# Matmuls moved into the waits of five norms, and one unit for both context query tiles in differential attention

## The chip, the cores and the metric

The kernel runs on one NeuronCore of a Trainium2 chip, in one launch. The metric is device time in microseconds, the median over runs; less is better. The engines are TensorE (PE in the rows: matmuls, with PEld for its weight loads), VectorE (DVE), ScalarE (ACT), GpSimd (POOL) and SyncE (SP), which issues most DMAs. A matmul accumulates in a PSUM bank; the other engines read it from there.

## The reference

Two transformer layers in sequence over a latent `h` of 256 tokens by 1024, all in float32. The first block is a convolution and retention mixer, a feed-forward part and a gated projection of a side input `p`, each closed by an RMS norm that is added to the residual:

```
x = x + rmsnorm(concat(y_conv, y_ret) @ w_out, mix_post_norm)
h = rmsnorm(x, ffn_pre_norm)
x = x + rmsnorm((silu(h @ w_ffn_gate) * (h @ w_ffn_up)) @ w_ffn_down, ffn_post_norm)
e = sigmoid(x @ w_ple_gate) * (p @ w_ple_proj)
x = x + rmsnorm(e, ple_post_norm)
```

The second block has two layers over the latent and over a context of 256 tokens, each with a modulated norm, attention, and a SwiGLU. Its first layer is differential attention with 8 heads of two 64-wide score maps; the latent's queries see context and latent keys (512), the context's queries see the context's keys (256):

```
p = softmax(q1 k1) - lam * softmax(q2 k2)          # per head, per query
y = rmsnorm(p @ v, subln) * (1 - lam_init) @ wo
h = h + g_m * y;  h = h + g_f * swiglu(modulate(rmsnorm(h)))   # and the same for ctx
```

The second layer is neighbourhood attention with 16 heads of 64 over the latent, followed by the same kind of SwiGLU and a last norm.

## The kernel before

**Matmuls.** Every float32 weight block is loaded by SP (`raw`), and split into two rounded parts: `hi` by a cast on ACT (L130), `lo` by a subtraction on DVE (L131). The buffers of `hi` and `lo` are five each, of 1024 columns. Activations are split in the same way. A product is then three matmuls, hi·hi, hi·lo and lo·hi, for each of its 8 blocks of 128 rows (`mm3`, L169 to L171; with tokens on the output's partitions `mm3_tok`, L196 to L198). 24 matmuls make one 128x256 output, 48 a bank of 512 columns.

**Norms.** A norm over 1024 features runs across partitions. `Stat.add` squares a tile on ACT (L226, L229) and adds it on DVE (L231). `rstd` sums over partitions by matmuls with a column of ones (L242), scales on DVE (L212), raises to the power -1/2 on POOL (L213), and broadcasts the result over the partitions by matmuls (L248). `post_norm` then makes, for each of 8 tiles, a product and a sum on DVE (L553, L554), a hi part on ACT (L148 or L152) and a lo part on DVE (L149 or L153), on which the next matmuls wait. `norm_mod` does the same with a modulation (DVE L639, ACT L642, DVE L643).

**Order.** The instructions are written in Python in program order; the framework's scheduler orders each engine's queue and places waits. `tc.issue_after(ins)` holds what is written in its block behind `ins` in that order. Around the change, the program goes: input products; `pp`, the product of `p` with `w_ple_proj` (48 matmuls, 12 for each of four banks of the ring `mm`, copied out at L531); the output projection `w_out` (192 matmuls); its norm; the feed-forward part; three blocks of the second layer's `wqkv` for the context (`early_some(0, 3)`, 48 matmuls each); `post_norm` into `o`; the gate `w_pg` (192 matmuls) with the product `e`; the `early` rest; the norm of `e`; the norm of layer two; then differential attention.

**Differential attention.** `da_unit` handles one tile of 128 queries of one head: two score maps in two PSUM banks (L781, 64 rows of weights), a maximum over each (DVE L788), an exponential with its sum (ACT L790), a reciprocal and two combinations on DVE (L794 to L796), transposes (L799), a copy (L801), the product with v (L806), and a norm of its own with ACT and POOL (L809 to L813). 8 heads have 2 latent and 2 context units each, 32 in all. Between units, `fill_in` places projection pieces of the next heads. The next unit's scores wait until both banks are free (`both_free`).

**After attention.** `wo_piece` and `wo_rest` apply the output projection for latent (v=0) and context (v=1) and add to the residual (L958); `ffn_norm` and `ffn_first` are the norm and the first four banks of the following SwiGLU (24 matmuls for each bank and v).

**Neighbourhood attention.** At L1119 each of 8 pairs of heads multiplies probabilities with values in 8 pairs of matmuls that use 64 columns of the array each, over four blocks of keys.

Of the kernel before, what the change touches and what calls it, by code (L numbers as in the profile page):

```python
# [14 lines left out]
P = 128  # L15
# [19 lines left out]
EARLY = 3, 3  # L35
# [27 lines left out]
def body(ctx, tc, a):  # L63
# [151 lines left out]
    class Stat:  # L215
# [5 lines left out]
        def add(self, src):  # L221
# [13 lines left out]
        def rstd(self, r=None, columns=False, keep=True):  # L235
# [11 lines left out]
            for t in range(nt):  # L247
                pe.matmul(pb[:, t * P:(t + 1) * P], v[:, t:t + 1].to_broadcast([P, P]), ident, start=True, stop=True)  # L248
# [171 lines left out]
    sm = tmp1("sm", 1)  # L420
# [144 lines left out]
    def out_proj(name, xs, base):  # L565
# [3 lines left out]
        for c in range(4):  # L569
# [24 lines left out]
    for j in range(KF):  # L594
        w = w_blocks(a["ffn1"][j])
# [77 lines left out]
    def early_qk(c, grp):  # L673
# [695 lines left out]
```

## Time and profile before

| | |
|---|---|
| median of 3 runs | 1416.42 us (1415.89 to 1419.45) |
| the profiled execution's own time | 1422.92 us |
| its span, first to last instruction | 1421.1 us |
| mean granted TensorE clock | 0.983 |
| PE busy | 1377.3 us, 97% |
| DVE busy | 1077.5 us, 76% |
| ACT busy | 698.6 us, 49% |
| POOL busy | 66.8 us, 5% |
| DMA | 239.76 MB, mean 169 GB/s |

The chain of work that ended last runs over PE for 91% of the span. The profile's 40 slices show PE busy nine tenths or more nearly everywhere; the stretches below that are short, and a table of 20 us stretches shows them better than the slices do. A row of the trace gives start and duration in us, the engine, line and operation, and in brackets the idle time before it with what ended it. One matmul's duration overlaps the next one's; the distance between starts is what it costs.

### The profile page before, as it was taken

What the parts mean: (1) busy time and instruction counts of PE and PEld (TensorE: products, weight loads), DVE (VectorE), ACT (ScalarE), POOL (GpSimd) and SP (SyncE); (2) the same over time, 40 slices, a digit from 0 to 9 for tenths busy, and PEclk for the clock granted to TensorE, in tenths of its full rate; (3) what the DMA queues carried; (4) which work ended last, traced back from release to release, by engine and by line L of the source; (5) the groups of instructions that cost most, each with busy time, mean ns of one, the idle gap of its engine ahead of it and who ended that gap; (6) DMA issues with size and microseconds to landing.
All of it is one profiled execution on the core that took longest, in us unless ns stands there. A gap on an engine that the chain in (4) does not pass through costs nothing.

```text
span 1421.1 us, 24831 instructions
## 1 busy us (share of the span) xinstructions
PE 1377.3 (97%) x9465; PEld 1240.0 (87%) x9465; DVE 1077.5 (76%) x2198; ACT 698.6 (49%) x1323; POOL 66.8 (5%) x119
## 2 busy tenths in 40 slices
PE   6999899999998999999999999999999999999997
PEld 6899799999997899799888888888997878888886
DVE  6875799986576788977699999974754556797764
ACT  5656544454365778664422222223544445655442
POOL 0000000000000223220000000000000000000000
PEclk9999899999999999999999999999999999999999
DMA  8356498667354234234465676643632223455563
GB/s 287 113 185 226 172 321 295 221 206 223 132 195 159 94 121 129 80 103 163 133 219 182 210 250 216 213 143 109 192 131 87 93 80 116 135 191 190 157 179 98
DMA packets 78311, 239.76 MB, mean 169 GB/s; under 512 B 8816, under 2 KB 14192, under 8 KB 78064
## 3 DMA queue, kind: packets, MB, share of 16 engines
q1 hardware_dynamic: 77760, 237.79, 51.8%
q8 instruction: 74, 1.21, 0.4%
q10 hardware_dynamic: 432, 0.39, 0.1%
q14 instruction: 45, 0.37, 0.1%
HBM read 237.10 MB, written 1.05 MB: 168 GB/s over the span
## 4 chain that ended last, share of the span: by engine, by line
PE 91%; DVE 2%; ACT 2%; DMA 2%; issue 1%; POOL 1%; SPq 0%; POOLq 0%; ACTq 0%; DVEq 0%
PE mm L169 20%; PE mm L170 19%; PE mm L171 19%; PE mm L181 5%; PE s L181 2%; PE mm L183 2%; PE mm L196 2%; PE mm L197 2%; PE mm L198 2%; PE s L781 1%; PE o L1119 1%; PE s L171 1%; PE s L170 1%; PE s L169 1%; PE t L806 1%; PE s L1079 1%
## 5 line engine op out<-in xcount | busy, mean ns | idle before, releaser
L130 ACT CAST hi<-raw 128x1024 fp32r<-128x1024 f32 (+2 forms) x382 | 365.1, 958 | 514.8 <-PE mm L170 280.5
L131 DVE TENSOR_TENSOR lo<-raw,hi 128x1024 fp32r<-128x1024 f32 (+2 forms) x382 | 422.6, 1108 | 170.3 <-ACT hi L130 166.0
L169 PE MATMUL mm<-x,hi 128*128 128x256 f32 (+2 forms) x1444 | 454.8, 319 | 15.8 <-ACT x L152 7.8
L170 PE MATMUL mm<-x,hi 128*128 128x256 f32 (+2 forms) x1444 | 454.2, 316 | 1.4 <-DVE x L643 1.3
L171 PE MATMUL mm<-x,lo 128*128 128x256 f32 (+2 forms) x1444 | 453.3, 315 | 0.8 <-DVE lo L131 0.8
L169 PEld LDWEIGHTS mm<-x,hi 128*128 128x128 f32 x1444 | 278.7, 195 | 45.1 <-issue 16.0
L171 PEld LDWEIGHTS mm<-x,lo 128*128 128x128 f32 x1444 | 280.5, 194 | 18.4 <-issue 3.4
L170 PEld LDWEIGHTS mm<-x,hi 128*128 128x128 f32 x1444 | 280.7, 195 | 17.6 <-issue 1.7
L282 DVE SCALAR_TENSOR_TENSOR junk<-adaw,sb 128x512 f32<-128x512 f32 x320 | 220.2, 688 | 11.8 <-DMA adaw<-ada 7.3
L169 PE MATMUL mm<-o,hi 128*128 128x256 f32 (+1 forms) x284 | 84.9, 306 | 2.3 <-ACT o L148 2.1
L171 PE MATMUL mm<-o,lo 128*128 128x256 f32 (+1 forms) x284 | 85.9, 304 | 0.0
L170 PE MATMUL mm<-o,hi 128*128 128x256 f32 (+1 forms) x284 | 85.7, 303 | 0.0
L213 POOL TENSOR_TENSOR rv<-rv,mhalf 128x2 f32<-128x2 f32 (+1 forms) x16 | 14.5, 906 | 1203.5 <-DVE rv L212 1203.5
L196 PE MATMUL mm<-hi,x 128*128 128x256 f32 x240 | 70.1, 292 | 0.0
L198 PE MATMUL mm<-hi,x 128*128 128x256 f32 x240 | 69.1, 288 | 0.0
L197 PE MATMUL mm<-lo,x 128*128 128x256 f32 x240 | 68.9, 287 | 0.0
L170 PE MATMUL mm<-q,hi 128*128 128x256 f32 (+1 forms) x195 | 61.2, 314 | 0.0
L171 PE MATMUL mm<-q,lo 128*128 128x256 f32 (+1 forms) x195 | 61.1, 313 | 0.0
L169 PE MATMUL mm<-q,hi 128*128 128x256 f32 (+1 forms) x195 | 61.1, 313 | 0.0
L169 PEld LDWEIGHTS mm<-o,hi 128*128 128x128 f32 x284 | 54.2, 194 | 6.0 <-ACT o L148 2.8
L171 PEld LDWEIGHTS mm<-o,lo 128*128 128x128 f32 x284 | 55.2, 194 | 2.5 <-issue 0.8
L170 PEld LDWEIGHTS mm<-o,hi 128*128 128x128 f32 x284 | 55.2, 194 | 1.7
(288 smaller groups left out, 2386.9 us busy)
## 6 DMA issues: line engine op xcount, KB each, us to landing
raw<-gu SPq DMA_DIRECT2D x88, 512.0 KB, 4.5
adaw<-ada SPq DMA_DIRECT2D x80, 512.0 KB, 4.5
raw<-wqkv SPq DMA_DIRECT2D x72, 512.0 KB, 4.0
raw<-ffn SPq DMA_DIRECT2D x44, 512.0 KB, 5.5
raw<-down SPq DMA_DIRECT2D x37, 384.0 KB, 3.2
raw<-down SPq DMA_DIRECT2D x37, 320.0 KB, 3.0
raw<-w_in SPq DMA_DIRECT2D x22, 512.0 KB, 5.2
o<-ada SPq DMA_DIRECT2D x32, 256.0 KB, 5.7
```

The source lines that it names most:

```text
L130: last_conv[:] = [act.copy(hi[:, :n], raw[:, :n]).ins, dve.tensor_tensor(lo[:, :n], raw[:, :n], f32(hi[:, :n]), op=ALU.subtract).ins]
L131: dve.tensor_tensor(lo[:, :n], raw[:, :n], f32(hi[:, :n]), op=ALU.subtract).ins]
L169: pe.matmul(out, wh, xh, start=first and k == 0, stop=False)
L170: pe.matmul(out, wh, xl, start=False, stop=False)
L171: last_mm[0] = pe.matmul(out, wl, xh, start=False, stop=last and k == n - 1).ins
L181: last_mm[0] = pe.matmul(out, wh, x, start=first and k == 0, stop=end).ins
L183: last_mm[0] = pe.matmul(out[:, :T], wl, x[:, :T], start=False, stop=False).ins
L196: pe.matmul(out, xh[:, ts_], wh, start=k == 0, stop=False)
L197: pe.matmul(out, xh[:, ts_], wl, start=False, stop=False)
L198: pe.matmul(out, xl[:, ts_], wh, start=False, stop=k == n - 1)
L213: pool.tensor_tensor(out, out, mhalf[:, :n], op=ALU.pow)
L282: dve.scalar_tensor_tensor(out=junk, in0=raw[:, gs_], scalar=1.0, in1=sb[:, v, gs_], op0=ALU.mult, op1=ALU.mult, accum_out=acc[:, n, v, g: ...
```

## The change

Four edits. First, `rstd` takes a pair `fill`: one function is called behind the sum matmuls, one behind the broadcast matmuls, and each writes matmuls there. Second, work is cut and handed to it: `pp` into four pieces of 12 matmuls, moved from before `w_out` to behind it; the 9 context blocks of `wqkv` into 36 quarters of 12, dealt out by `FILLS`; the pieces of `wo` for v=1 and of `ffn_first(0)`. Third, `da_unit` takes one or two query tiles: the two context tiles of a head become one unit with 512 columns per bank. Fourth, the order of the key blocks and of the two heads at L1119 is reversed. `w_pp` now keeps 2 of the 5 weight buffers from the input products until the norm behind `w_out`, and the first two `ffn1` blocks are written behind that projection's last square and sum.

```diff
+FILLS = 6, 1, 5, 3, 1, 12, 1, 5, 99
@@ Stat.rstd
+            if fill:
+                fill[0](mm.ins)
             v = small.tile([P, 4], F32, tag="rv", name="rv", bufs=4)
             inv_sqrt(v[:, :nt], ps[:, :nt], 1.0 / self.of)
...
+            if fill:
+                fill[1](mm.ins)
@@ after the input products
-    w = per_k(weights(a["w_pp"], (1024, 1024)), (8, 8), P)
...
-    for c in range(4):
-        ps = bank(pmm, "mm")
-        for j in range(2):
-            n = 2 * c + j
-            mm3(ps[:, j * T:(j + 1) * T], w[2 * n:2 * n + 2], px)
-        s = slot("pt")
-        act.activation(s, ps, AF.Copy, scale=0.5)
-        pp.append(s)
+    w_pp = per_k(weights(a["w_pp"], (1024, 1024)), (8, 8), P)
@@ behind out_proj
+    def pp_piece(ins):
+        c = len(pp)
+        ps = bank(pss, "s")
+        with behind(ins):
+            for j in range(2):
+                n = 2 * c + j
+                mm3(ps[:, j * T:(j + 1) * T], w_pp[2 * n:2 * n + 2], px)
...
     blocks, st = out_proj("w_out", ys, V_MIXPOST)
-    xs, st = post_norm(blocks, st, "x", V_FFNPRE)
+    pp_piece(last_mm[0])
+    xs, st_x = post_norm(blocks, st, "x", V_FFNPRE, (pp_piece, lambda ins: [pp_piece(ins) for _ in range(2)]))
+
+    with tc.issue_after(st.last_sq), tc.issue_after(st.last_add):
+        w_next = [w_blocks(a["ffn1"][j]) for j in range(2)]
@@ before post_norm "o", and the two norms behind it
-    early_some(0, EARLY[0])
+    fill(FILLS[0])(None)
+    xs, _ = post_norm([blocks[n // 2][:, (n % 2) * T:(n % 2 + 1) * T] for n in range(KD)], st, "o",
+                      fill=(fill(FILLS[1]), fill(FILLS[2])))
...
-        early_some(EARLY[0], EARLY[1])
-    r = st.rstd(keep=False)
+    fill(FILLS[3])(last_mm[0])
+    r = st.rstd(keep=False, fill=(fill(FILLS[4]), fill(FILLS[5])))
...
-    r = st.rstd(keep=False)
+    r = st.rstd(keep=False, fill=(fill(FILLS[6]), fill(FILLS[7])))
-    early_some(EARLY[1] if EARLY[1] is not None else EARLY[0], 99)
@@ da_unit (qts is (0,), (1,) for the latent, (0, 1) for the context)
-            dve.tensor_reduce(out=sc[:, 2 + m:3 + m], in_=o, axis=AX.X, op=ALU.max, negate=True)
+            dve.tensor_reduce(out=nmax[:, m, :nq], in_=ps[m].rearrange("p (u n) -> p u n", u=nq), axis=AX.X, op=ALU.max, negate=True)
             e = tmp2("e", 3)
-            act.activation(e[:, :n], o, AF.Exp, bias=sc[:, 2 + m:3 + m], accum_out=sc[:, 4 + m:5 + m])
+            for u in range(nq):
+                us = slice(u * n, (u + 1) * n)
+                act.activation(e[:, us], ps[m][:, us], AF.Exp, bias=nmax[:, m, u:u + 1], accum_out=sums[:, m, u:u + 1])
@@ behind attention
-    ffn_norm(0)
-    wo_first(1)
+    wo_some(1, (0, 1))(None)
+    ffn_norm(0, (wo_some(1, (2,)), wo_some(1, (3, 4, 5, 6, 7))))
...
-    ffn_first(0)
-    ffn_norm(1)
-    ffn_first(1)
+    ffn_first(0, (0,))(None)
+    ffn_norm(1, (ffn_first(0, (1,)), ffn_first(0, (2, 3))))
+    ffn_first(1, (0, 1, 2, 3))(None)
@@ na_heads
-            for kt in range(4):
-                for jj in range(2):
+            for kt in (3, 2, 1, 0):
+                for jj in (1, 0):
```

PE's queue at the norm behind `w_out`, before: `mm_1673` is the last bank of `w_out`, `t` the norm's two small products, `mm_1872` the first bank of the feed-forward part.

```order
L171 MATMUL mm_1673<-x_1449,lo_1668 128x256
L242 MATMUL t_1730<-ones_100,acc_1514 128x1 x2
L242 MATMUL t_1730<-ones_100,sq_1727 128x1 x2
L248 MATMUL t_1738<-tab_98,rv_1735 128x128 x2
L169 MATMUL mm_1872<-x_1744,hi_1860 128x256
```

The same place in the changed kernel, with four pieces of `pp` (`s_1670`, `s_1690`, `s_1711`, `s_1726`), of 12 matmuls each:

```order
L171 MATMUL s_1670<-x_1152,lo_1349 128x256
L245 MATMUL t_1685<-ones_100,acc_1454 128x1 x2
L245 MATMUL t_1685<-ones_100,sq_1666 128x1 x2
L169 MATMUL s_1690<-x_1152,hi_1348 128x256
...
L254 MATMUL t_1708<-tab_98,rv_1705 128x128 x2
L169 MATMUL s_1711<-x_1152,hi_1354 128x256
...
L169 MATMUL s_1726<-x_1152,hi_1354 128x256
...
L169 MATMUL mm_1884<-x_1744,hi_1811 128x256
```

One piece stands ahead of the sum, one between sum and broadcast, two behind the broadcast.

DVE's queue at the same norm, before, from the last weight part to the norm's first finished tile:

```order
L131 TENSOR_TENSOR lo_2023<-raw_2024,hi_2022 128x1024
L231 TENSOR_TENSOR acc_1514<-acc_1514,sq_1723 128x256
L212 TENSOR_SCALAR rv_1735<-t_1730 128x2
L553 TENSOR_TENSOR t1_1741<-q_1465,t_1738 128x256
L553 TENSOR_TENSOR t1_1749<-q_1465,t_1738 128x256
L554 TENSOR_TENSOR h0_85<-h0_85,t1_1741 128x256
L554 TENSOR_TENSOR h1_86<-h1_86,t1_1749 128x256
L153 SCALAR_TENSOR_TENSOR x_1744<-h0_85,vec_97,x_1744 128x256
```

And in the changed kernel:

```order
L234 TENSOR_TENSOR acc_1454<-acc_1454,sq_1663 128x256
L215 TENSOR_SCALAR rv_1705<-t_1685 128x2
L131 TENSOR_TENSOR lo_1812<-raw_1813,hi_1811 128x1024
L131 TENSOR_TENSOR lo_1818<-raw_1819,hi_1817 128x1024
L550 TENSOR_TENSOR t1_1741<-q_1405,t_1708 128x256
L550 TENSOR_TENSOR t1_1749<-q_1405,t_1708 128x256
L131 TENSOR_TENSOR lo_1824<-raw_1825,hi_1823 128x1024
L551 TENSOR_TENSOR h0_85<-h0_85,t1_1741 128x256
L551 TENSOR_TENSOR h1_86<-h1_86,t1_1749 128x256
L131 TENSOR_TENSOR lo_1830<-raw_1831,hi_1829 128x1024
L153 SCALAR_TENSOR_TENSOR x_1744<-h0_85,vec_97,x_1744 128x256
```

The weight parts of the feed-forward blocks, before the norm's sum until now, stand between the norm's own steps; a fifth one, `lo_2023`, follows four tiles later.

PE's queue from the norm of `e` to layer two's first products, before (`acc_4809` is the sum for `e`, `acc_5037` that for layer two, `x_5091` its first normed tile):

```order
L170 MATMUL s_5206<-x_3965,hi_5194 128x256
L242 MATMUL t_5023<-ones_100,acc_4809 128x1 x2
...
L248 MATMUL t_5031<-tab_98,rv_5028 128x128 x2
L196 MATMUL s_5269<-hi_5257,x_3935 128x256
...
L242 MATMUL t_5080<-ones_100,acc_5037 128x1 x2
...
L248 MATMUL t_5088<-tab_98,rv_5085 128x128 x2
L169 MATMUL mm_5526<-x_5091,hi_5520 128x256
```

In the changed kernel (`x_5443` is the first normed tile):

```order
L171 MATMUL s_5023<-x_3950,lo_5031 128x256
L245 MATMUL t_5072<-ones_100,acc_4809 128x1 x2
...
L254 MATMUL t_5094<-tab_98,rv_5091 128x128 x2
L169 MATMUL s_5097<-x_3935,hi_5098 128x256
...
L245 MATMUL t_5332<-ones_100,acc_5289 128x1 x2
L169 MATMUL s_5337<-x_3935,hi_5338 128x256
...
L254 MATMUL t_5365<-tab_98,rv_5362 128x128 x2
L169 MATMUL s_5337<-x_3955,hi_5338 128x256
...
L169 MATMUL mm_5500<-x_5443,hi_5494 128x256
```

The first sum moved from behind 68 matmuls (two blocks and 20 of the second) to behind 36; behind the second broadcast stand now 60 matmuls (`s_5337`, 36, and `s_5406`, 24), where before `mm_5526` followed at once.

## Rows read from the trace of the kernel before

**Rows 1.** the page's busy time: us, share of the span, instructions
```profile
PE 1377.3 (97%) x9465; PEld 1240.0 (87%) x9465; DVE 1077.5 (76%) x2198; ACT 698.6 (49%) x1323; POOL 66.8 (5%) x119
```

**Rows 2.** busy us by 20 us stretch: length, engines with their instructions, PEclk, DMA
```profile
140.00:160.00 20.00, 13.79 (x89) 13.28 (x90) 13.02 (x34) 9.58 (x25) 0.69 (x1) 0.74 0.34 137
...
360.00:380.00 20.00, 17.22 (x128) 16.84 (x127) 10.67 (x19) 8.16 (x12) 0.69 (x1) 0.85 0.50 165
...
440.00:460.00 20.00, 14.97 (x104) 13.83 (x105) 15.98 (x34) 10.14 (x18) 0.00 (x0) 0.90 0.41 128
...
640.00:660.00 20.00, 20.00 (x169) 19.95 (x168) 18.42 (x38) 11.63 (x20) 0.57 (x1) 1.00 0.68 232
...
660.00:680.00 20.00, 17.86 (x125) 17.48 (x124) 10.31 (x25) 4.96 (x11) 0.70 (x1) 0.83 0.18 58
```

**Rows 3.** the timeline, w_out's inputs to normed tiles: start, us, what, [idle, releaser]
```profile
112.68 1.23 ACT L515 ACTIVATE pt<-t,rv 128x128 f32<-128x128 f32 x4
...
139.41 0.28 PE L171 MATMUL mm<-x,lo 128*128 128x256 f32 x1
...
140.61 1.04 ACT L130 CAST hi<-raw 128x1024 fp32r<-128x1024 f32 x1 [1.97 <-DMA raw<-ffn]
...
141.69 1.23 DVE L131 TENSOR_TENSOR lo<-raw,hi 128x1024 fp32r<-128x1024 f32 x1 [1.79 <-ACT hi L130]
...
143.39 0.98 PE L242 MATMUL t<-ones,acc 128*128 128x1 f32 x4 [3.70 <-DVE acc L231]
...
146.33 1.23 PE L248 MATMUL t<-tab,rv 128*128 128x128 f32 x4 [1.10 <-POOL rv L213]
...
149.27 1.01 PE L169 MATMUL mm<-x,hi 128*128 128x256 f32 x3 [1.72 <-ACT x L152]
...
158.49 0.48 DVE L153 SCALAR_TENSOR_TENSOR x<-h,vec,x 128x256 fp32r<-128x256 f32 x1 [0.24 <-ACT x L152]
```

**Rows 4.** the timeline of PE at post_norm into o
```profile
374.08 1.22 PE L248 MATMUL t<-tab,rv 128*128 128x128 f32 x4 [1.16 <-POOL rv L213]
...
376.92 1.01 PE L169 MATMUL mm<-o,hi 128*128 128x256 f32 x3 [1.61 <-ACT o L148]
```

**Rows 5.** the timeline from w_pg's last matmul to attention's first scores
```profile
401.67 0.28 PE L171 MATMUL mm<-o,lo 128*128 128x256 f32 x1
...
406.98 0.42 DVE L231 TENSOR_TENSOR acc<-acc,sq 128x256 f32<-128x256 f32 x1
...
440.75 0.50 PE L169 MATMUL mm<-x,hi 128*128 128x256 f32 x2 [1.58 <-ACT x L642]
...
442.79 0.58 PE L170 MATMUL mm<-x,hi 128*128 128x256 f32 x1 [1.29 <-DVE x L643]
...
457.82 0.50 PE L781 MATMUL s<-o 64*128 64x512 f32 x2 [2.44 <-ACT o L148]
```

**Rows 6.** the timeline at the norm of the context behind attention
```profile
663.28 0.48 DVE L643 SCALAR_TENSOR_TENSOR x<-t,mod,x 128x256 fp32r<-128x256 f32 x1
...
668.64 0.16 DVE L212 TENSOR_SCALAR rv<-t 128x2 f32<-128x2 f32 x1 [4.87 <-PE t L242]
...
669.63 0.71 PE L248 MATMUL t<-tab,rv 128*128 128x128 f32 x4 [1.03 <-POOL rv L213]
```

**Rows 7.** PE's waits: us in total, times, longest
```profile
PE s L781 <- ACT e L790: 2.1, 3, 0.8
```

**Rows 8.** attention's groups, 455 to 645 us: count, busy us, mean ns, idle before
```profile
L788 DVE TENSOR_REDUCE sc<-s 128x1 f32<-128x512 f32 x32 | 21.0, 684 | 3.8 <-PE s L781 3.4 <-POOL sc L811 0.5
...
L788 DVE TENSOR_REDUCE sc<-s 128x1 f32<-128x256 f32 x32 | 12.4, 418 | 2.4 <-PE s L781 2.4
...
L790 ACT ACTIVATE e<-s,sc 128x256 f32<-128x256 f32 x32 | 15.1, 475 | 2.7 <-DVE sc L788 1.7 <-DVE e L796 0.8
```

**Rows 9.** the timeline of PE at one run of L1119
```profile
1080.22 0.65 PE L1119 MATMUL o<-pt,adaw 128*64 128x256 f32 x2
...
1081.11 1.94 PE L1119 MATMUL o<-pt,adaw 128*64 128x256 f32 x14
```

More of the change, by code (lines that the diff above doesn't have):

```diff
@@ L189, in halves, with mm3_tok @@
         return t
-    def mm3_tok(out, w, xs, ts_):
+    def mm3_tok(out, w, xs, ts_, first=True, last=True):
         n = len(xs)
@@ L195, in mm3_tok, with behind @@
             (wh, wl), (xh, xl) = w[k], xs[k]
-            pe.matmul(out, xh[:, ts_], wh, start=k == 0, stop=False)
+            pe.matmul(out, xh[:, ts_], wh, start=first and k == 0, stop=False)
             pe.matmul(out, xh[:, ts_], wl, start=False, stop=False)
-            pe.matmul(out, xl[:, ts_], wh, start=False, stop=k == n - 1)
+            last_mm[0] = pe.matmul(out, xl[:, ts_], wh, start=False, stop=last and k == n - 1).ins
     CS = (slice(0, P), slice(P, 2 * P))
+    def behind(ins):
+        return tc.issue_after(ins) if ins is not None else nullcontext()
     def part(xs, v):
@@ L810, in da_unit @@
-        pool.tensor_scalar(out=sc[:, 10:11], in0=sc[:, 6:7], scalar1=128 * EPS, scalar2=sc[:, 9:10], op0=ALU.mult, op1=ALU.add)
-        pool.tensor_tensor(sc[:, 10:11], sc[:, 10:11], mhalf[:, :1], op=ALU.pow)
-        on = tmp.tile([P, P], F32, tag="on", name="on", bufs=2)
-        act.activation(on, po[:, :P], AF.Copy, scale=sc[:, 10:11])
+        for u in range(nq):
+            for j in range(nk):
+                kt = j + (2 if ctx_q else 0)
+                vv = v[kt // 2][:, (kt % 2) * T + (hh % 2) * P:(kt % 2) * T + (hh % 2) * P + P]
+                jj = u * nk + j
+                mm = pe.matmul(po[:, u * P:(u + 1) * P], pT[:, jj * P:(jj + 1) * P], vv, start=j == 0, stop=j == nk - 1)
@@ L814, in da_unit @@
         flush()
-        late.append((po_all[:, at:at + P], on))
+        for u in range(nq):
+            late.append((po_all[:, ats[u]:ats[u] + P], on[:, u * P:(u + 1) * P]))
         return last_s
@@ L821, in body @@
     V = [[] for _ in range(4)]
-    def behind(ins):
-        return tc.issue_after(ins) if ins is not None else nullcontext()
     def qk_piece(c, grp, j):
@@ L991, in wo_piece, with wo_some, run @@
         return run
-    def wo_first(v):
-        for n in range(KD):
-            wo_piece(v, n)(None)
+    def wo_some(v, ns):
+        def run(ins):
+            for n in ns:
+                wo_piece(v, n)(ins)
+        return run
     da_heads(3, {u: [wo_piece(0, n) for n in ns] for u, ns in WO_AT.items()})
@@ L1009, in wo_rest, with ffn_norm, ffn_first, run @@
             resid(0, 2, n, o, v, sts)
-    def ffn_norm(v):
-        norm_mod(0, 3, xs, (h, hc)[v], sts[v].rstd(keep=False)[:, :T], v, v * T)
-    def ffn_first(v):
-        for ps, w in zip(firsts, w0):
-            mm3(ps[:, v * T:(v + 1) * T], w, part(xs, v))
+    def ffn_norm(v, fill=None):
+        norm_mod(0, 3, xs, (h, hc)[v], sts[v].rstd(keep=False, fill=fill)[:, :T], v, v * T)
+    def ffn_first(v, ns):
+        def run(ins):
+            for n in ns:
+                with behind(ins):
+                    mm3(firsts[n][:, v * T:(v + 1) * T], w0[n], part(xs, v))
+        return run
     wo_rest(0)
-    ffn_norm(0)
-    wo_first(1)
+    wo_some(1, (0, 1))(None)
+    ffn_norm(0, (wo_some(1, (2,)), wo_some(1, (3, 4, 5, 6, 7))))
     wo_rest(1)
@@ L1084, in na_softmax @@
     def na_softmax(ps, qt, bt):
[L1085 removed]
+        sc = small.tile([P, 16], F32, tag="sc", name="sc", bufs=8)
         b0 = 128 if qt == 0 else 0
```

160 lines of the change are left out of this document (88 added, 72 removed).

## The prediction

> **What bounds the kernel now.** I read the busy times first: PE is busy 97% of the span, DVE 76%, ACT 49% [rows 1]. So time is to be had from stretches in which PE's 3% is lost, and from those in which PE is counted busy but goes slowly. The table of 20 us stretches shows both [rows 2]: an undisturbed stretch holds 169 matmuls, one per 20 / 169 = 0.118 us; four others hold 89, 128, 104 and 125, at a granted clock of 0.74 to 0.90. There the clock was for a part of the stretch at 1.2 of 2.4 GHz, each time after a wait of PE. The missing matmuls times 0.118 us are what a stretch lost, waits and slow clock together: 80 (9.4 us), 41 (4.8), 65 (7.7), 44 (5.2). Then I read the timeline of each: in every one PE stands at a norm, and the last wait is for the first normed tile or for the tiles behind it [rows 3 to 6]. Attention loses less, by waits for the softmax [rows 7].
>
> **The change, part by part.**
>
> *The norm behind `w_out`.* Before, `w_out` ends at 139.41; a cast that waited 1.97 us for a weight stands on ACT ahead of the squares; the sum starts at 143.39, the broadcast at 146.33, the first fed matmul at 149.27, and the last normed tile is there at 158.49 + 0.48 = 158.97 [rows 3]. Until then PE is fed by one tile at a time. The change takes 48 matmuls of `pp`, 48 x 0.118 = 5.7 us, from ahead of `w_out` and puts them here, so `w_out` could end 5.7 us earlier. But those 48 covered something: the scaling of retention's output on ACT runs until 112.68 + 1.23 = 113.91 [rows 3], and `w_out` needs it. The 192 matmuls of `w_out` take 22.7 us, so it began near 116.7 and can begin near 111.0 now; 14 of its matmuls (1.7 us) don't need that output, and then PE waits from 112.7 to 113.9, and for the transposes, a product and a split behind. The wait is 1.2 us without those and 4 with them in full; I take 2.8. `w_out` then ends at 139.41 - 5.7 + 2.8 = 136.5. The sum comes 1.7 us behind (a square and an addition that no cast holds up; a piece of `pp`, 12 x 0.118 = 1.4, lies beside it), at 138.2. From there the tiles, not PE, set the end: before, sum to last tile took 158.97 - 143.39 = 15.6. Five subtractions L131 of 1.23 us each now stand in DVE's chain, as its order shows. Two fit where DVE waits for sum and broadcast; three are added, 3.7. The sum at full clock gives back 0.8, since between sum and broadcast 2.94 us were spent at the slow clock. The last tile comes at 138.2 + 15.6 + 3.7 - 0.8 = 156.7, 2.3 us sooner. So -2.3; the ends are -5.7 (nothing uncovered, two subtractions more hidden) and 0 (all five in the chain).
>
> `w_pp` also holds 2 of 5 weight buffers during `w_out`. Three remain; one block of `w_out` is 24 matmuls, 2.8 us, its cast and subtraction 1.04 + 1.23 = 2.3 us [rows 3]. This fits, if the loads are in time: at nothing, and 8 blocks x 1.5 us = 12 if each refill is uncovered by about half a block.
>
> *`post_norm` into `o`.* PE waited 1.16 us for the broadcast and 1.61 for the first tile, and then ran slowly [rows 4]. Twelve matmuls (1.4 us) now lie in the first gap and 60 (7.1 us) behind the broadcast, ahead of the first `w_pg` matmul; the first tile took 376.92 - 374.08 = 2.8 us from the broadcast, so several tiles wait when PE comes. All 4.8 us go; I see no late party, the weights of the two blocks being the same as before: -4.8 (-4.0 to -5.5).
>
> *`e`'s norm, layer two's norm, and the first scores.* From 440 to 460 us 65 matmuls are missing, 7.7 us: the waits of 1.58, 1.29 and 2.44 us [rows 5] and the slow clock after them. Six of its matmuls are scores 512 wide, worth two each: 7.0. Now 60 matmuls stand behind the second broadcast, and two quarters of the last context block among the first projections, so those three waits go. The price is at the other end. Before, 68 matmuls separated `w_pg`'s end (401.67) from the sum of `e`; now 36 do, 36 x 0.118 = 4.2 us, to 406.2. The last addition for it ends at 406.98 + 0.42 = 407.4 [rows 5], so PE now waits 1.2 to 1.4 us. Net 7.0 - 1.4 = -5.6. The ends: -7.7 (the addition comes sooner, and the whole loss goes) and -3 (the wait also puts the clock down, for as long as behind 440.75).
>
> *The norm of the context behind attention.* This stretch lost 5.2 us, and DVE stood 4.87 us for PE's sum [rows 6]: 96 matmuls of `ffn_first(0)` were queued ahead of it. Now 24 are, and 72 (8.5 us) lie in the gaps. But the 24 of one bank need all 8 tiles of the latent, and DVE finishes the last at 663.28 + 0.48 = 663.76, in work that isn't moved. Before, PE filled the time until then with four banks tile by tile. Now it has one bank and the `wo` matmuls, and waits there some 5 us instead. The loss moves: 0, with -5.2 (the tiles come sooner, as fewer residual sums stand before them) and +3 (wait plus slow clock) as ends.
>
> *Attention.* A context head had four maxima of 418 ns on DVE and has two of 684: 1.67 - 1.37 = 0.30 us less [rows 8], and half the small steps. For 8 heads that is over 2.4 us of DVE. PE waits for the exponentials only 2.1 us in all [rows 7]. The exponentials stay at four per head, but one unit now holds both banks for all four. I take the loss named in the wait row as gone: -2. The ends are -4 and +5: twice the saving on DVE, and half of 8 x (2 x 0.475 + 0.266) = 9.7, the time by which a context unit's chain grows (two more exponentials, and 684 for 418).
>
> *Neighbourhood attention.* A run of 16 matmuls at L1119 is split: 2, then 14, with one ordinary matmul between, 0.89 us from start to start and 1.94 for the rest [rows 9]. A run of x pairs costs a fixed part and a part per pair: (1.94 - 0.65) / 6 = 0.215 per pair and 0.65 - 0.215 = 0.43 fixed; less the tail of the last matmul, which overlaps what follows, I take 0.36. Eight runs become whole: 8 x 0.36 = -2.9. The ends: -4.3 (8 x 0.54, with the odd matmul's slot) and -1 (other pairs, of score matmuls, are split more by the new order).
>
> The Trainium skill, in TensorEngine Tiling (Array Packing), section Key Properties, says that a change of tiling mode drains TensorE. The rows of L1119 agree as to a fixed cost. It speaks against a gain from the merged units on PE: the order shows 31 visits to the 64-row scores for 32 before, so by it 0.4 us would be saved, not 8 visits' 2.9.
>
> **Sum.** -2.3 - 4.8 - 5.6 + 0 - 2 - 2.9 = -17.6 us. The profiled execution took 1422.92 us, 1.8 over its span, and 6.5 over the median of the runs; it would come to 1405.3. I subtract the same from the median: 1416.42 - 17.6 = 1398.8.
>
> **Rivals.**
>
> *DVE and ACT are the bound at the norms, and the fillers only move the wait.* For it: DVE is at 18.42 of 20 us in the stretch before 660 [rows 2], and five subtractions enter a chain on DVE. Against it: at `post_norm` into `o` DVE is at 10.67 of 20. Then the first term is 0, the third -3, the fourth +2: 0 - 4.8 - 3 + 2 - 2 - 2.9 = -10.7, 1405.7.
>
> *All holes close.* For it: DVE's idle 4.87 us [rows 6], which the earlier sum takes away. Then the first and fourth terms are at their lower ends: -5.7 - 4.8 - 5.6 - 5.2 - 2 - 2.9 = -26.2, 1390.2. Against it: both need tiles of DVE that aren't moved.
>
> *The weight buffers.* `w_out` on three buffers loses 12 us: -17.6 + 12 = -5.6, 1410.8. Against it: 2.3 us of work per 2.8 us of matmuls.
>
> *Slower: the context's double units hold both banks.* The next unit's scores can't start until four exponentials are done. Two maxima and four exponentials are 2 x 0.684 + 4 x 0.475 = 3.3 us [rows 8]; if no projection piece covers them, that is 8 x 3.27 = 26.1 us, against 15.6 from the other terms: +10.5, 1426.9. It decides from 15.6 / 8 = 2.0 us uncovered per head. For it: that wait is there already, three times. Against it: its longest is 0.8 us.
>
> **Chances.** Forecast 0.50, DVE bound 0.21, all holes close 0.15, buffers 0.08, slower 0.06. The range goes from 1386 to 1411: some 4 us below the case of closed holes, for the lower ends of the other terms, and up to the buffers' case. About 0.3%, 4.2 us, is what a measurement of this kernel can tell from no change. Faster by more than that, below 1412.2: the first three and a part of the buffers' case, 0.88; within it 0.06, the rest of that case and of the forecast's upper tail; slower 0.06.
>
> **What would show it.** Stretches like those of the second group, with 160 matmuls or more at clock 1.00 around the norm into `o` and between layer two's norm and the first scores, show these terms right. In the first stretch the last L153 of the norm should come about 2.3 us sooner; a first w_out matmul that waits on ACT or DVE shows the lost cover. A wait of PE of 1 to 1.5 us at `e`'s sum, and one near 5 us ahead of the context's sum, should appear. The output products of neighbourhood attention should stand in eight runs of 16 in one piece. The prediction is wrong if waits for the exponentials grow past 2 us per head, or if `w_out` waits for its weights.

## The result, and the profile after

The changed kernel took 1406.29 us (median of 6 runs, 1403.37 to 1409.82) beside 1418.10 for the kernel before; the ratio is 0.9906, 95% interval [0.9889, 0.9922], or -13.3 us (-15.7 to -11.1). Measured a second time beside other kernels it came to 0.9887 [0.9871, 0.9902], -16.0 us. The forecast was -17.6.

The profiled execution took 1403.65 us, with a span of 1401.9. Its busy row, which answers to [rows 1]:

```profile
PE 1367.0 (98%) x9465; PEld 1231.6 (88%) x9465; DVE 1072.5 (77%) x2166; ACT 695.8 (50%) x1315; POOL 61.6 (4%) x119
```

PE's share rose by one point; DVE and ACT hardly moved. The same 20 us stretches as in [rows 2], from the changed kernel (length, engines with their instructions, PEclk, DMA):

```profile
140.00:160.00 20.00, 18.06 (x129) 14.95 (x127) 17.77 (x40) 13.61 (x31) 0.70 (x1) 1.00 0.44 154
...
360.00:380.00 20.00, 19.49 (x162) 19.28 (x162) 13.98 (x30) 8.06 (x15) 1.58 (x1) 1.00 0.39 129
...
440.00:460.00 20.00, 19.52 (x161) 17.98 (x160) 17.52 (x33) 13.30 (x33) 3.54 (x8) 1.00 0.58 189
...
640.00:660.00 20.00, 17.34 (x115) 16.85 (x116) 12.03 (x29) 5.48 (x13) 0.69 (x1) 0.83 0.22 78
```

The first three now hold 129, 162 and 161 matmuls for 89, 128 and 104, at clock 1.00. In the fourth, 640 to 660, stood 169 matmuls before; now there are 115 at 0.83. Since the broadcast of this norm comes 17.9 us sooner (651.78 for 669.63), this is the place of the row of 660 to 680 before (125 at 0.83): the hole behind attention is still there.

To see where the time went I cut both traces at the same four places: the broadcast of the second norm, ahead of all that was edited; the broadcast of the norm of the context behind `w_out`; the first scores; the first output product of neighbourhood attention. The rows in the changed kernel:

```profile
94.95 0.60 PE L254 MATMUL t<-tab,rv 128*128 128x128 f32 x4
...
172.13 0.60 PE L254 MATMUL t<-tab,rv 128*128 128x128 f32 x4
...
443.93 0.96 PE L810 MATMUL s<-o 64*128 64x512 f32 x6
...
1064.24 1.95 PE L1161 MATMUL o<-pt,adaw 128*64 128x256 f32 x16
```

With the same rows of the other kernels (of before: 98.03, 176.46, 457.82 and 1080.22, the last two in [rows 5, 9]), the differences make the stages below, in us; the columns add up to the span. Timed: the ratio to the kernel before, less one, times 1418. The last two stages hold more than their names say: that of attention goes on through the feed-forward part behind it.

| kernel | timed | start | `w_out` and its norm | three norms, to first scores | attention and context norm | neighbourhood attention to end |
|---|---|---|---|---|---|---|
| before | 0 | 98.03 | 78.43 | 281.36 | 622.40 | 340.9 |
| changed | -13.3 | 94.95 | 77.18 | 271.80 | 620.31 | 337.7 |
| changed, second time | -16.0 | 95.18 | 75.26 | 273.34 | 620.30 | 337.7 |
| before, NA order only | -4.7 | 97.23 | 77.44 | 281.52 | 621.48 | 336.7 |
| before, double units only | +2.7 | 95.55 | 78.81 | 281.70 | 624.09 | 341.0 |
| changed, context norm as before | -18.3 | 94.90 | 75.70 | 273.36 | 618.06 | 336.6 |
| changed, no quarters | -5.5 | 98.24 | 76.00 | 282.17 | 622.76 | 336.3 |
| changed, single units | -13.0 | 97.93 | 75.70 | 273.36 | 623.12 | 338.0 |
| changed, two banks by tile | -20.0 | 93.56 | 77.47 | 273.35 | 615.60 | 336.5 |
| changed, pp put back | -16.3 | 96.07 | 79.68 | 271.83 | 615.72 | 337.9 |
| both of the last two | -18.7 | 93.70 | 80.39 | 271.80 | 614.46 | 336.6 |
| changed, first weights free | -18.6 | 94.34 | 73.20 | 271.71 | 622.29 | 338.0 |
| changed, FILLS 4 and 11 | -21.8 | 94.44 | 77.36 | 271.69 | 616.78 | 336.2 |
| three of these together | -25.7 | 94.31 | 75.00 | 271.56 | 614.31 | 337.8 |

The first column of stages is the same work in all 14 profiles and still reaches from 93.56 to 98.24: a profile pair differs there by chance, and the pair before/changed by 3.1 us, which is no part of the change. Without it the pair differs by 19.2 - 3.1 = 16.1 us. The pair is a wide one besides: before was profiled in an execution of 1422.92 us (median 1418.10), the changed kernel in one of 1403.65 (median 1406.29).

Much of the gain is clock. The granted clock, averaged over the timed runs, was 0.9853 in 29 runs of the kernel before and 0.9905 in the changed kernel; what is missing to 1, times the mean times of 1418.6 and 1406.2 us, is 20.8 and 13.4 us. In the second measurement it is 21.6 and 11.2 us. By this estimate 7 to 10 us of the 13 to 16 are clock that was not lost. It is an upper one, since a slow clock costs nothing while PE waits. What is left, some 5 us or more, is about what the new order in neighbourhood attention gives alone (-4.7).

### The profile page after: what moved, and what is told of

Its sections match the earlier page's. It is cut to its first block, busy times and chain, and to the rows that moved or that the text cites. A ratio compares the mean times of both kernels' runs of the same rounds, so it can differ in the third digit from the quotient of the medians.

```text
span 1401.9 us, 24781 instructions
## 1 busy us (share of the span) xinstructions
PE 1367.0 (98%) x9465; PEld 1231.6 (88%) x9465; DVE 1072.5 (77%) x2166; ACT 695.8 (50%) x1315; POOL 61.6 (4%) x119
## 4 chain that ended last, share of the span: by engine, by line
PE 90%; DVE 4%; ACT 2%; DMA 1%; issue 1%; POOL 1%; SPq 0%; POOLq 0%; DVEq 0%; ACTq 0%
PE mm L169 20%; PE mm L170 19%; PE mm L171 19%; PE mm L181 5%; PE s L181 2%; PE mm L183 2%; PE mm L196 2%; PE mm L198 2%; PE mm L197 2%; DVE lo L131 2%; PE s L810 1%; PE t L841 1%; PE s L1120 1%; PE s L169 1%; PE s L170 1%
## 5 line engine op out<-in xcount | busy, mean ns | idle before, releaser
L169 PE MATMUL mm<-x,hi 128*128 128x256 f32 (+2 forms) x1428 | 448.4, 317 | 10.8 <-ACT x L152 7.0
L170 PE MATMUL mm<-x,hi 128*128 128x256 f32 (+2 forms) x1428 | 448.4, 315 | 4.3 <-DVE x L660 3.5
L171 PE MATMUL mm<-x,lo 128*128 128x256 f32 (+2 forms) x1428 | 447.4, 314 | 0.8 <-DVE lo L131 0.7
L169 PEld LDWEIGHTS mm<-x,hi 128*128 128x128 f32 x1428 | 274.1, 193 | 38.3 <-issue 15.0
L170 PEld LDWEIGHTS mm<-x,hi 128*128 128x128 f32 x1428 | 275.1, 193 | 22.2 <-DVE x L660 4.1
L171 PEld LDWEIGHTS mm<-x,lo 128*128 128x128 f32 x1428 | 275.4, 193 | 18.7 <-issue 3.3
L290 DVE SCALAR_TENSOR_TENSOR junk<-adaw,sb 128x512 f32<-128x512 f32 x320 | 220.3, 689 | 13.3 <-DMA adaw<-ada 8.8
```

The source lines that it names most:

```text
L169: pe.matmul(out, wh, xh, start=first and k == 0, stop=False)
L170: pe.matmul(out, wh, xl, start=False, stop=False)
L171: last_mm[0] = pe.matmul(out, wl, xh, start=False, stop=last and k == n - 1).ins
L290: dve.scalar_tensor_tensor(out=junk, in0=raw[:, gs_], scalar=1.0, in1=sb[:, v, gs_], op0=ALU.mult, op1=ALU.mult, accum_out=acc[:, n, v, g: ...
```

## The experiments

**The order in neighbourhood attention alone** (on the kernel before).

```diff
-            for kt in range(4):
-                for jj in range(2):
+            for kt in (3, 2, 1, 0):
+                for jj in (1, 0):
```

> The kernel before with one edit: the order of key blocks and heads in neighbourhood attention's output products is reversed. If a split run costs a fixed part each time (0.36 us by the prediction), eight whole runs give -2.9 us; the trace of the changed kernel lost 4.2 us less in that stage, so the range is -2.9 to -4.2 us against before. Rival: PE's order there is off the path, since softmax on DVE and ACT sets it; then 0, and the runs are whole in the trace without any change of the stage.

Measured: 0.9967 [0.9954, 0.9979], -4.7 us (-6.5 to -3.0). PE's row where [rows 9] had two:

```profile
1077.68 1.95 PE L1119 MATMUL o<-pt,adaw 128*64 128x256 f32 x16
```

Sixteen records, of eight matmuls, in one piece of 1.95 us. Before, from the start of the first two to the end of the last it took 1081.11 + 1.94 - 1080.22 = 2.83, with one ordinary matmul (0.12) inside: 0.76 us more for this run. The rival falls: the stage is 4.2 us shorter too. The gain is a little above the -2.9 to -4.2 that was expected.

**The double units alone** (on the kernel before: `da_unit` of the changed kernel, `for qts in ((0, 1),) if ctx_q else ((0,), (1,))`).

> The kernel before with one edit: the two context tiles of a head are one unit, 24 units for 32. The prediction took -2 us; the traces of before and after differ by 4.3 us of lost TensorE time between the first scores and the last product with v. Theory: -2 to -4.3 us against before. Rival 1: the gain in that stretch came from the fillers ahead of it, which start attention at full clock; then -0.5 us or nothing here. Rival 2: a unit that holds both banks for four exponentials makes PE wait, +2 to +5 us.

Measured: 1.0019 [1.0008, 1.0029], +2.7 us, and 1.7 in the stage of attention. Two stretches, with the second also as it was in the kernel before, and two rows of PE's waits:

```profile
440.00:460.00 20.00, 17.31 (x106) 15.95 (x107) 13.94 (x29) 9.16 (x16) 0.06 (x1) 0.76 0.41 129
...
580.00:600.00 20.00, 17.14 (x108) 14.59 (x108) 18.06 (x48) 11.37 (x33) 4.99 (x11) 0.83 0.33 99
```

```profile
580.00:600.00 20.00, 17.91 (x121) 14.49 (x122) 18.57 (x48) 12.61 (x38) 5.99 (x13) 0.91 0.31 100
```

```profile
PE t L808 <- DVE e L805: 1.9, 1, 1.9
...
PE s L786 <- ACT e L796: 0.4, 1, 0.4
```

The size is that of rival 2, at its lower end, but not its mechanism: PE's wait at the scores for the exponentials shrank from 2.1 us [rows 7] to 0.4. One transpose waits 1.9 us for the combination of the exponentials instead, and from 580 to 600 108 matmuls run at clock 0.83, for 121 at 0.91 before. The timed runs fit a cost by the clock: their mean is 0.9832 in 12 runs, for 0.9853 before, and 0.0021 x 1420 us is 3.0 us. Which wait set it is not shown.

**The context's norm behind attention put back** (on the changed kernel).

```diff
-    wo_some(1, (0, 1))(None)
-    ffn_norm(0, (wo_some(1, (2,)), wo_some(1, (3, 4, 5, 6, 7))))
+    ffn_norm(0)
+    wo_some(1, range(KD))(None)
...
-    ffn_first(0, (0,))(None)
-    ffn_norm(1, (ffn_first(0, (1,)), ffn_first(0, (2, 3))))
+    ffn_first(0, (0, 1, 2, 3))(None)
+    ffn_norm(1)
```

> The changed kernel with one part undone: behind attention, all of wo for v=1 stands behind the norm of v=0, and all 96 matmuls of ffn_first(0) ahead of the sum of v=1, tile by tile over four banks, with no fillers, as before. The prediction had this part at 0; the trace shows 1.7 us more lost than before. Theory (the wait only moved to the latent's tiles): 0 to -2 us against the changed kernel, some -13 to -15 us against before. Rival (the fillers hid the norm's chain): 3 to 5 us slower than the changed kernel.

Measured: 0.9871 [0.9854, 0.9888], -18.3, which is 5.0 us better than the changed kernel's first measurement and 2.3 better than its second (these two intervals overlap); the stage is 2.25 us shorter. The rival falls. By the stage, and by the first measurement, this part of the change costs time.

**The quarters undone** (on the changed kernel).

```diff
-FILLS = 6, 1, 5, 3, 1, 12, 1, 5, 99
+FILLS = 12, 0, 0, 0, 0, 0, 0, 0, 99
-    for f in (qk_piece(0, 0, 0), qk_piece(0, 1, 0), fill(FILLS[8]), v_piece(0, 0), v_piece(0, 1)):
+    for f in (fill(FILLS[8]), qk_piece(0, 0, 0), qk_piece(0, 1, 0), v_piece(0, 0), v_piece(0, 1)):
```

> The changed kernel with the quarters undone: three whole context blocks ahead of the norm into o, no fillers inside that norm and the two behind w_pg, the other six blocks ahead of the first projections of attention as before. Theory (the fillers close the holes at these three norms): 9 to 10.5 us slower than the changed kernel, so -3 to -4 us against before; stretches with clock 1.2 GHz reappear at the norm into o and behind layer two's norm. Rival (DVE and ACT are the bound, fillers only move waits): within 3 us of the changed kernel.

Measured: 0.9961 [0.9949, 0.9973], -5.5: 7.8 or 10.5 us slower than the changed kernel by its two measurements, and 10.4 in the stage of the three norms. Its stretches, and two rows of PE's waits:

```profile
360.00:380.00 20.00, 17.19 (x130) 16.91 (x129) 12.53 (x26) 7.37 (x12) 0.69 (x1) 0.91 0.46 150
...
440.00:460.00 20.00, 17.31 (x104) 15.95 (x105) 14.14 (x29) 8.82 (x14) 0.00 (x0) 0.76 0.39 128
...
580.00:600.00 20.00, 17.13 (x108) 14.53 (x107) 18.48 (x50) 10.93 (x32) 4.93 (x11) 0.83 0.32 99
```

```profile
PE s L810 <- ACT o L148: 2.4, 1, 2.4
...
PE mm L169 <- ACT x L659: 1.6, 1, 1.6
```

130 and 104 matmuls, as in [rows 2], and the waits of [rows 5]. The third stretch is like that of the double units alone: without the quarters, attention loses clock there too, at 0.83 where the changed kernel has 1.00 in every 20 us stretch from 440 to 640.

**Single units in the changed kernel** (`da_unit` and its calls as before).

> The changed kernel with one part undone: 32 units of one query tile each in differential attention. Alone, the double units made the kernel before 2.7 us slower (ratio 1.0019). Theory A (parts add up): this is 2 to 3 us faster than the changed kernel, -15 to -16 us against before. Theory B (the double units gain only behind the fillers, since the profile loses 4.0 us in attention with both and 10.1 with the units alone): 2 to 3 us slower than the changed kernel, -10 to -11 us against before.

Measured: 0.9908 [0.9892, 0.9925], -13.0, the same as the changed kernel's first measurement and 3.0 us short of its second. The stage of attention is 2.8 us longer, which theory B expected, but one profile's clock can make that: it was granted 0.91 from 560 to 580 and 0.74 from 640 to 660, for 1.00 and 0.83 in the changed kernel, or (0.09 + 0.09) x 20 = 3.6 us. From 560 to 580 it also fell in the profile of the next kernel, which has double units. So neither theory is borne out; what can be said is that alone the double units cost, and that behind the fillers no cost of theirs is seen.

**Two banks by tile at the context's norm** (on the changed kernel; `ffn_first` takes a range of tiles `ks`, `both` calls two functions).

```diff
-    ffn_first(0, (0,))(None)
-    ffn_norm(1, (ffn_first(0, (1,)), ffn_first(0, (2, 3))))
+    ffn_first(0, (0, 1))(None)
+    ffn_norm(1, (ffn_first(0, (2,), (0, 4)), both(ffn_first(0, (2,), (4, KD)), ffn_first(0, (3,)))))
```

> The changed kernel with another order behind attention: two banks of ffn_first(0), 48 matmuls, are fed tile by tile ahead of the sum of v=1, 12 matmuls stand between sum and broadcast, 36 behind the broadcast. Theory (the one bank ahead of the sum starves on the latent's tiles, the clock falls, and the 24 matmuls ahead of the broadcast then delay it): the waits of 1.8 us at the tiles shrink to under 1 us, and the kernel is 4 to 6 us faster than the changed one, level with the old order or up to 1.5 us better (-18 to -20 us against before). Rival (tiles of DVE rule whatever is queued): no better than the changed kernel.

Measured: 0.9859 [0.984, 0.9877], -20.0, and 4.7 us less in the stage. Stretch, waits and the norm's sum and broadcast:

```profile
640.00:660.00 20.00, 18.11 (x150) 17.69 (x149) 12.58 (x29) 6.85 (x16) 0.69 (x1) 1.00 0.26 94
```

```profile
PE mm L170 <- DVE x L660: 1.9, 2, 1.3
```

```profile
646.16 0.50 PE L245 MATMUL t<-ones,acc 128*128 128x1 f32 x4
...
648.96 0.60 PE L254 MATMUL t<-tab,rv 128*128 128x128 f32 x4
```

150 matmuls at clock 1.00 for 115 at 0.83. Two waits for tiles are left, of 0.6 and 1.3 us for 1.8 and 1.7, so not quite as small as expected; the broadcast comes 2.80 us behind the sum, for 6.17 in the changed kernel. The theory holds; its two parts, more banks ahead of the sum and fewer matmuls behind it, were not tried apart.

**pp put back ahead of `w_out`** (on the changed kernel; the four pieces are again one loop in the ring `mm`).

> The changed kernel with the pieces of pp put back ahead of w_out, in the ring mm, and no fillers in the norm behind w_out; the first feed-forward weights stay behind the last square. Theory (the term of -2.3 us, a wait of 2.8 us at the transposes against 5.7 us of filled holes): 2 to 3 us slower than the changed kernel, about -11 us against before; the wait at the transposes is gone. Rival (the five subtractions in DVE's chain take all of it back): 0, or 1 us faster.

Measured: 0.9885 [0.9868, 0.9902], -16.3. Neither expectation: the stage of `w_out` is 2.5 us longer, as the theory said, but attention's is 4.6 us shorter, at a place that wasn't edited. The reason is in PE's queue there:

```profile
PE mm L170 <- DVE x L655: 0.3, 1, 0.3
```

```profile
643.96 0.58 PE L245 MATMUL t<-ones,acc 128*128 128x1 f32 x4 [0.20 <-DVE acc L234]
...
649.63 0.60 PE L254 MATMUL t<-tab,rv 128*128 128x128 f32 x4
```

The scheduler had put the context's sum behind 10 of the first bank's 24 matmuls, where 22 stood before it in the changed kernel, and let two banks alternate behind it; the waits for tiles shrank from 3.5 us to 0.3. That the broadcast came 5.67 us behind the sum didn't make the stage longer: PE worked all but 1.0 us of it. So this run says nothing on `pp` in its total, and was followed by the next one.

**Both: pp back, and two banks by tile.**

> The kernel with the new order behind attention (two banks tile by tile), and with pp put back ahead of w_out. Putting pp back alone came out 3 us faster than the changed kernel, but its queue behind attention had also changed: the sum of the context's norm stood earlier and two banks alternated. With that place given the same order, theory (moving pp gains 2 to 3 us) expects it 2 to 3 us slower than the new order with pp moved, about -17.5 us against before. Rival (moving pp costs time): 2 to 3 us faster than that, -22 to -23.

Measured: 0.9868 [0.9852, 0.9884], 1.3 us slower than two banks alone, with intervals that overlap. The stage of `w_out` is 2.9 us longer (80.39 for 77.47), that of attention 1.1 shorter. The stage bears the theory out; the total points the same way and doesn't prove it.

**The first feed-forward block's weights not held back** (on the changed kernel).

```diff
+    w_next = [w_blocks(a["ffn1"][0])]
     with tc.issue_after(st.last_sq), tc.issue_after(st.last_add):
-        w_next = [w_blocks(a["ffn1"][j]) for j in range(2)]
+        w_next.append(w_blocks(a["ffn1"][1]))
```

> The changed kernel with one edit: the first feed-forward block's two weights are no longer held behind w_out's last square and sum, only the second block's. Two of the five subtractions L131 then stand ahead of the norm's sum, so DVE's chain from sum to last tile is 2 x 1.14 = 2.3 us shorter. Theory (DVE's chain sets the last tile): last normed tile 2.3 us sooner behind the sum, kernel 1.5 to 2.5 us faster than the changed one. Rival (PE has other work left, or the cast delays the squares): 0.

Measured: 0.9869 [0.9851, 0.9887], -18.6; the stage is 2.1 us shorter than in the changed kernel's second profile, and 4.0 shorter than in its first, which lost clock there (0.72 granted from 110 to 116 us). But not by what was expected. Sum and last tile, first of this kernel, then of the changed one's second run:

```profile
132.79 0.50 PE L245 MATMUL t<-ones,acc 128*128 128x1 f32 x4
...
149.57 0.48 DVE L153 SCALAR_TENSOR_TENSOR x<-h,vec,x 128x256 fp32r<-128x256 f32 x1 [0.24 <-ACT x L152]
```

```profile
133.63 0.50 PE L245 MATMUL t<-ones,acc 128*128 128x1 f32 x4
...
150.90 0.48 DVE L153 SCALAR_TENSOR_TENSOR x<-h,vec,x 128x256 fp32r<-128x256 f32 x1
```

From sum to last tile 149.57 + 0.48 - 132.79 = 17.3 us, for 17.8: 0.5 less, not 2.3. The theory, that DVE's chain sets the last tile, falls. What changed is how much PE does meanwhile; two stretches of each, in the same order:

```profile
140.00:150.00 10.00, 9.06 (x65) 7.85 (x64) 9.66 (x25) 6.27 (x17) 0.00 (x0) 1.00 0.38 134
...
150.00:160.00 10.00, 10.00 (x76) 7.94 (x79) 7.17 (x13) 5.93 (x13) 0.87 (x1) 1.00 0.44 137
```

```profile
140.00:150.00 10.00, 8.37 (x57) 6.99 (x55) 10.00 (x25) 6.50 (x16) 0.00 (x0) 1.00 0.58 207
...
150.00:160.00 10.00, 9.82 (x70) 7.78 (x71) 6.97 (x14) 6.89 (x16) 0.70 (x1) 1.00 0.27 87
```

141 matmuls for 127. Between PE's short waits for tiles stand 19, 18 and 18 matmuls from 141 us on, in the changed kernel 12, 22 and 18. This fits weights of the third bank that are ready earlier, so that the first tiles feed three banks where they fed two; no run shows that by itself.

**One quarter more ahead of `e`'s sum** (`FILLS = 6, 1, 5, 4, 1, 11, 1, 5, 99`).

> The changed kernel with FILLS 6, 1, 5, 4, 1, 11, 1, 5, 99: one more quarter ahead of e's sum, one less behind its broadcast. Theory: PE's wait of 1.2 to 1.3 us at that sum goes, and the kernel gains 1 to 1.3 us, less than timing can tell. Rival (the chain behind that sum rules): it only moves the wait to the next sum, 0.

Measured: 0.9846 [0.9833, 0.9859], -21.8, far more than expected. The stage with the edit gained at most 1.7 us (271.69 for 273.34, and 0.1 against the first profile). The two differ by the clock: the wait at `e`'s sum is 1.18 us in both, and in the second profile the clock behind it was granted 0.72 from 396 to 402 us, in the first 1.00 from 397 to 403. Of the eight profiles with that wait four have such a fall behind it; of the three without the wait, none. The rest, 3.5 us, is again in the stage behind: as with `pp` put back, the scheduler had moved the context's sum forward, to 639.99 here. The one edit had an effect of its own and another by accident.

**Three together** (two banks by tile, first weights free, one quarter more), and the changed kernel once more beside it.

> The changed kernel with three edits: two banks tile by tile behind attention, the first feed-forward block's weights not held back, and one more quarter ahead of e's sum. Theory (each removes its own wait): -6.5 from the first, -2.3 to -3.5 from the second, -1.2 from the third, so 10 us faster than the changed kernel and 23 to 25 us faster than before, near 1394. Rival (the gains share one cause, the clock behind attention): no better than the first edit alone, -20 us.

> The changed kernel once more, unedited, beside the others of this job, to tighten its interval. Theory: 0.989 to 0.992 of the kernel before, with spans that differ by several us with the clock granted at the norm behind attention.

Measured: 0.9819 [0.9806, 0.9832], 1394.38 us, -25.7; the changed kernel beside it 0.9887, -16.0. The four stretches:

```profile
140.00:160.00 20.00, 19.05 (x135) 15.76 (x134) 17.18 (x40) 13.71 (x31) 0.90 (x1) 1.00 0.47 176
...
360.00:380.00 20.00, 20.00 (x170) 20.00 (x169) 13.88 (x29) 9.75 (x17) 0.00 (x0) 1.00 0.38 124
...
440.00:460.00 20.00, 19.52 (x159) 17.45 (x158) 17.33 (x35) 14.92 (x36) 3.53 (x8) 1.00 0.49 155
...
640.00:660.00 20.00, 19.91 (x167) 19.71 (x166) 14.16 (x28) 9.87 (x16) 0.69 (x1) 1.00 0.27 91
```

135, 170, 159 and 167 matmuls, all at clock 1.00. This version beats both kernels; the three edits together gave 9.7 us, and 10 were expected. By the stages, against the second profile of the changed kernel, the shares are 0.3, 1.8 and 6.0 us. The last is not the two banks' alone: the scheduler moved the context's sum forward here too, and 30 matmuls stand between it and its broadcast, 4.9 us:

```profile
638.05 0.50 PE L245 MATMUL t<-ones,acc 128*128 128x1 f32 x4
...
642.95 0.60 PE L254 MATMUL t<-tab,rv 128*128 128x128 f32 x4
```

## Why the prediction was right, and where it was off

That matmuls moved into the norms' waits gain time, in part by the clock, came true, and so did the three norms and their price at `e`'s sum. The total of -17.6 for -13.3 and -16.0 owes something to luck as well: three of the six terms were off by some 2 us, in both directions, and a fourth came out near for a wrong reason.

*The norm behind `w_out`: -2.3 predicted, -1.3 in the pair of profiles, -3.2 in the second.* The two profiles differ by the clock: granted 0.72 from 110 to 116 us in the first, or 1.7 us, and 1.00 in the second. The steps can be followed one by one in the first. The transposes of retention's output with a matmul that waits for its weights, the sum and broadcast, and on DVE two weight parts in the wait, the last of those that stand in the chain, and the last tile:

```profile
108.41 0.44 PE L534 MATMUL t<-tab,x 128*128 128x128 f32 x2 [0.58 <-ACT x L523]
...
109.34 0.39 PE L169 MATMUL mm<-x,hi 128*128 128x256 f32 x1 [0.49 <-ACT hi L130]
...
110.38 0.44 PE L534 MATMUL t<-tab,pt 128*128 128x128 f32 x2 [0.32 <-ACT pt L523]
...
113.14 0.63 PE L534 MATMUL t<-tab,pt 128*128 128x128 f32 x2
...
135.31 0.50 PE L245 MATMUL t<-ones,acc 128*128 128x1 f32 x4
...
138.31 0.71 PE L254 MATMUL t<-tab,rv 128*128 128x128 f32 x4 [0.51 <-POOL rv L216]
```

```profile
136.47 2.36 DVE L131 TENSOR_TENSOR lo<-raw,hi 128x1024 fp32r<-128x1024 f32 x2
...
144.79 1.23 DVE L131 TENSOR_TENSOR lo<-raw,hi 128x1024 fp32r<-128x1024 f32 x1
...
152.59 0.49 DVE L153 SCALAR_TENSOR_TENSOR x<-h,vec,x 128x256 fp32r<-128x256 f32 x1
```

The lost cover is there, but smaller than the 2.8 us that I took: PE waits 0.58 and 0.32 us for the transposes, 0.49 for a weight between them, and the transposes drag on to 113.14, partly at the slow clock. From sum to last tile it took 152.59 + 0.49 - 135.31 = 17.8 us; predicted were 15.6 + 3.7 - 0.8 = 18.5. That this agrees is luck: with two subtractions fewer in the chain it took 17.3, so they don't cost 1.23 us each. Nor do the tiles set the end, as I had it: with the first weights free the last tile came 0.5 us sooner, counted from the start of the stage (55.7 for 56.2 in the changed kernel's second profile), and the stage was 2.1 us shorter. What does set the last tile stays open. The kernel also writes both squares of a bank of `w_out` ahead of its two copies on ACT, which no run has by itself. The weight buffers' rival, 12 us, didn't occur: 0.49 us is PE's only wait for a weight here.

*The three norms: -4.8 and -5.6 predicted, together -10.4; -9.6 and -8.0 measured, and 10.4 when undone.* The price at `e`'s sum, predicted at 1.2 to 1.4 us:

```profile
398.55 0.61 PE L245 MATMUL t<-ones,acc 128*128 128x1 f32 x4 [1.18 <-DVE acc L234]
```

1.18 us, for DVE's addition. The waits of 1.58, 1.29 and 2.44 us [rows 5] are gone. The -8.0 is the profile in which the clock fell behind this wait: the end that I had given to that, in a milder form (1.7 us).

*Attention, -2, and the context's norm, 0: -2.1 measured together, but both were mis-sized.* Their sum was right by luck, because two errors cancelled. With the context's norm as before, the stage is 622.40 - 618.06 = 4.3 us shorter. But the double units weren't worth 2 us of it: alone they cost 2.7. What attention gained goes with the fillers ahead of it, without which the same units lose it again (622.76 for 620.31 in the stage, clock 0.83 from 580 to 600). The prediction named the fillers' clock only up to the first scores. And at the context's norm the step that failed is "The loss moves: 0". It moved, as said, to the latent's tiles, but it grew:

```profile
640.97 0.39 PE L170 MATMUL mm<-x,hi 128*128 128x256 f32 x1 [1.76 <-DVE x L660]
...
643.28 0.39 PE L170 MATMUL mm<-x,hi 128*128 128x256 f32 x1 [1.70 <-DVE x L660]
...
645.61 0.85 PE L245 MATMUL t<-ones,acc 128*128 128x1 f32 x4
...
651.78 0.60 PE L254 MATMUL t<-tab,rv 128*128 128x128 f32 x4
```

```profile
644.99 0.49 DVE L660 SCALAR_TENSOR_TENSOR x<-t,mod,x 128x256 fp32r<-128x256 f32 x1
...
652.42 1.66 DVE L656 SCALAR_TENSOR_TENSOR t<-hc,mod,t 128x256 f32<-128x256 f32 x4 [4.92 <-PE t L254]
```

PE waits 1.76 and 1.70 us for two tiles, 3.5 where I had 5. Then its clock falls to half, and the 24 matmuls that stand between sum and broadcast run there: the broadcast comes 651.78 - 645.61 = 6.2 us behind the sum. So DVE stands for 4.92 us, as it stood 4.87 before [rows 6], now for the broadcast in place of the sum. The term is +2.3 by the stage, and +2.3 to +5.0 by the timed runs with this part put back; the end of +3 that I had given to a wait with a slow clock lies among these.

*Neighbourhood attention: -2.9 predicted, -4.7 alone, -3.2 in the pair to the end.* That a split run costs was right; the way I priced it was not. I read the 2 and 14 records as one pair and seven. But a run is eight matmuls, four key blocks for two heads, which the trace shows as two records each, and the first two records are both of one head. By my model the whole run takes 0.43 + 8 x 0.215 = 2.15 us; it takes 1.95, as long as the 14 alone (1.94 [rows 9]). In the trace the records of the two heads, on 64 columns each, start in twos 0.01 us apart; in the split run the first two and the last two stand alone. So the piece in front saves nothing behind. The ordinary matmul between the pieces:

```profile
1080.80 0.39 PE L197 MATMUL mm<-lo,x 128*128 128x256 f32 x1
```

The piece in front takes 1080.80 - 1080.22 = 0.58 us, and the ordinary matmul 0.31 where 0.118 is usual: 0.77 us for this run, and the same, 0.76 to 0.78, for seven of the eight, with one to fifteen ordinary matmuls between. Of it 2 x 0.215 = 0.43 is the one head's work alone; the other 0.34, for going in and out, is near my 0.36. Eight times 0.77 is 6.2 us; -4.7 (-6.5 to -3.0) was timed and -4.2 is in the stage, and what took the rest back isn't shown. The rule of the Trainium skill cited in the prediction (TensorEngine Tiling (Array Packing), Key Properties), that a change of tiling mode drains TensorE, agrees with the 0.34, not with the larger part.

*The rivals.* DVE as the bound fell for the three norms (no quarters: 8 to 10 us slower). At the context's norm its +2 was met, but not its reason: with two banks queued the same tiles of DVE leave waits of 1.9 us at clock 1.00. That all holes close came true in its total only with the three further edits. The slower rival, uncovered exponentials, was a wait of 2.3 us in all in the changed kernel, for 2.1 before [rows 7], now in seven pieces:

```profile
PE s L810 <- ACT e L820: 2.3, 7, 0.7
```

## What to carry to other kernels

Matmuls held back for a norm pay where PE would wait for the vector engines, and more where the clock falls behind such a wait. What counts is that they don't wait themselves: 24 matmuls between sum and broadcast took 6.2 us at a clock that had fallen just before, while in the fastest kernel 30 of them stand there, 4.9 us, at full clock and with the sum moved forward. Ahead of such a sum, feed as many banks as the tiles can keep busy, since one bank starves. Where a scheduler orders the queues, compare stages and not totals, with the granted clock of each: an edit in one place changed the order at another twice here, for 3.5 to 4.6 us, more than its own effect.

## What the runs showed of the hardware

- A run of 16 records on 64 columns took 1.95 us, as long as 14 of them whose first two had been split off (1.94): the two heads' halves start 0.01 us apart. The split cost 0.76 to 0.78 us in seven of eight runs, with one to fifteen full matmuls between.
- Two waits of 1.8 us, 0.6 us apart, were followed by a clock of 1.2 GHz (granted 0.83 over 640 to 660); with waits of 1.9 us in all at the same place it stayed at 1.00.
- One wait of 1.18 us at `e`'s sum, the same in eight profiles, had a clock of 1.2 GHz behind it in four of them, for 1.7 us of loss, and none in the other four.
- The first 95 us, the same in all kernels (738 matmul records), took from 93.56 to 98.24 us; a difference of 3 us between two profiles can lie wholly there.
